# A two-layer recurrent and attention block: the scan's triangle joints cut into pieces of 32 passes between other TensorE products

## The chip, the cores and the metric

The kernel runs on one NeuronCore of a Trainium2 chip. The metric is the device time of one execution, in microseconds (us). Three runs of the kernel before gave 5034.45 to 5045.35 us, median 5039.2 us.

## What is computed

The reference is a block of two layers over 2048 latent rows and 256 context rows of width 1024. Layer 0 is a recurrent mixer (16 heads of 64) that is scanned in both directions; layer 1 is a differential attention over 2304 keys. The change touches only the scan of layer 0, which per head and direction is

```
def step(S, inp):
    r_t, w_t, k_t, v_t, kk_t, a_t = inp
    sa = jnp.einsum("bhvk,bhk->bhv", S, kk_t)
    S = (S * w_t[:, :, None, :]
         - sa[..., None] * (kk_t * a_t)[:, :, None, :]
         + v_t[..., None] * k_t[:, :, None, :])
    return S, jnp.einsum("bhvk,bhk->bhv", S, r_t)
```

## The kernel before, in words

The program runs in phases: projections of layer 0 (`phase1`), the scans (`phase2`), the readout and the projections of layer 1, attention, and the last product. Only `phase2` differs.

`phase2` cuts the 2304 rows into 36 chunks of 64 and treats both directions of a chunk together. Inside a chunk the recurrence is a triangular system of 64 unknowns per head and direction. Its matrix is inverted in blocks: VectorE and GpSimd invert the 32x32 triangles on the diagonal (`invert`, two chunks at a time), four VectorE transposes unpack the result into `Tt` and `Dg` (`unpack`), and two small products of 32x32 blocks join the triangles. The first, `join_rows` (line 743), multiplies the off-diagonal block of `A` with `Tt` for two chunks at once (`w` = 0 and 1). The second, `join` (line 754), multiplies by `U`, which ScalarE has filled with `Dg` times -1 (line 759, four instructions), for one chunk. Each product of `join` or `join_rows` covers 16 heads and two 32x32 blocks; a float32 product is two passes of TensorE, so one joint of one chunk is 64 passes.

The loop variable `m` counts chunks whose scores are made, and `i = m - LEAD` is the chunk whose recurrence runs, five behind. One iteration, a step here, issues for each engine in this written order (`in_order` pins it):

- `chain(i)`, a generator in pieces: products of the state with QR (`xps` and `ops`); KB with RV, then RU with U into `chps` (its negation by ScalarE becomes the new RU, line 820); KB with RU into `xps` (line 825), after which VectorE updates the state `St` (lines 827 and 828); Pb with RU into `ops` (line 833), copied to RV by ScalarE (line 834) and stored. I call them KB·RU and Pb·RU. The first piece, KS with RV, is issued at the end of the step before.
- four groups of score products of chunk `m` (`order[0]` to `order[3]`, line 686, 32 passes each). Two go through `scores_k` (VectorE writes KS), two through `scores_b` (ScalarE copies A, VectorE writes Pb). Every group takes both buffers of the pool `sc` (tiles `scps`).
- eight transposes of BT by TensorE for each direction (`turn_keys`, tiles `chps`), copied to KB by ScalarE.
- the joints. In steps with odd `i` (the variable `even` in the code) it is both `join_rows`, so I call them Tt steps. In steps with even `i` (`odd` in the code) it is `join` of two chunks, one early and one late in the step: U steps. Their tiles are `chps`, in the pool `ch`.

The pools `sc` and `ch` have two buffers each, handed out in turn. SyncE's queue carries the loads of the next chunks and the stores of RV, spread by `pump` over the step. In the last five steps (`more` is false) no scores are left.

Of the kernel before, what the change touches and what calls it, by code (L numbers as in the profile page):

```python
# [11 lines left out]
F32 = mybir.dt.float32  # L12
# [21 lines left out]
def bcast(ap, dim, n):  # L34

    ap = ap.unsqueeze(dim)
    shape = list(ap.shape)
    shape[dim] = n
    return ap.broadcast_to(shape)
# [573 lines left out]
def phase2(k):  # L613
# [9 lines left out]
    with ExitStack() as st:  # L623
# [12 lines left out]
        sc = pool("p2sc", 2, space=PSUM)  # L636
        ch = pool("p2ch", 2, space=PSUM)
# [13 lines left out]
        def pump(n=1):  # L651

            for _ in range(min(n, len(queue))):
                traced = nc.cur_bb.bb.instructions
                queue.pop(0)()
                if i >= 0:
                    at = next(x for x in reversed(traced) if x.engine == mybir.EngineType.Activation)
                    k.tc.add_manual_dep(
                        traced[-1], at.name,
                        mybir.DependencyInfo(mybir.DependencyClass.Sync, mybir.DependencyReason.DATA),  # L660
                        reason="loads spread over the step")
# [76 lines left out]

        parts = ((slice(0, 32), slice(32, 64), slice(32, 64)), (slice(96, 128), slice(64, 96), slice(0, 32)))

        joint = lambda: ch.tile([128, 16, 32], F32, name="chps")

        def join_rows(A, par):

            cs = slice(16 * par, 16 * par + 16)
            ps = joint()
            for h in range(16):
                c = 16 * par + h
                for e, m, uc in parts:
                    nc.tensor.matmul(ps[m, h], A[e, c, uc], Tt[e, c], start=(h == 0), stop=True, skip_group_check=True)  # L750
            for e, m, uc in parts:
                nc.scalar.copy(Tt[m, cs], ps[m])

        def join(par):

            cs = slice(16 * par, 16 * par + 16)
            for g in range(4):
                r = lanes(g)
                nc.scalar.mul(U[r, cs, 32 * (g % 2):32 * (g % 2) + 32], Dg[r, cs], -1.0)
            yield  # L760
            ps = joint()
            for h in range(16):
                c = 16 * par + h
                for e, m, uc in parts:
                    nc.tensor.matmul(ps[e, h], Tt[m, c], U[m, c, uc], start=(h == 0), stop=True, skip_group_check=True)
            for e, m, uc in parts:
                nc.scalar.copy(U[e, cs, uc], ps[e])
            yield
# [9 lines left out]
        def chain(i, QR, KS, Pb, RV, KB):  # L778

            last = i + 1 == NCH  # L780
            par = i % 2
# [33 lines left out]
            for ab in range(2):  # L815
                for p in range(8):
                    for d in range(2):
                        h = 8 * ab + p
# [3 lines left out]
            if not last:  # L822
                for p, ab, h in heads:
                    for d in range(2):
                        add(pS[d][half[ab], p], KB[i, d][half[d], p, ab], RU[half[d], h], False, True)
                for d in range(2):
                    nc.vector.tensor_tensor(St[:, d], pS[d], St[:, d], op=ALU.add)
                    nc.vector.tensor_tensor(St[:, d], St[:, d], bcast(k.dec[:, d, ORDER[d][i]], 2, 64), op=ALU.mult)
            for ab in range(2):
                for p in range(8):  # L830
                    for d in range(2):
                        h = 8 * ab + p
                        add(po[ab][other[d], p], Pb[half[d], h], RU[half[d], h], False, True)
                nc.scalar.copy(RV[:, 8 * ab:8 * ab + 8], po[ab])
            for d in range(2):
                n = ORDER[d][i]
                (nc.sync if i + 2 < NCH else nc.scalar).dma_start(
                    out=S["o"][d, 64 * n:64 * n + 64].rearrange("t (h v) -> t h v", v=64), in_=RV[other[d]])
            yield

        step = lambda g: next(g, None)
        none = iter(())
        mk, mp = causal_masks(k, cx)
        QR, KS, Pb, BK, BT, RV, KB, A = {}, {}, {}, {}, {}, {}, {}, {}
# [27 lines left out]
        inv0, unp, joins, N, chains = none, none, [none, none], {}, {}  # L872

        with in_order(k, mybir.EngineType.PE, mybir.EngineType.DVE, mybir.EngineType.Activation, mybir.EngineType.Pool):
            for m in range(nch + LEAD):
                i, g = m - LEAD, m // 2
                more = m < nch
                par = m % 2

                def turn_keys(d):  # L880
                    if 0 <= i + 1 < nch:
                        KB[i + 1, d] = bt.tile(wide, F32, name=f"KB{d}")
                        turned(d, BT.pop((i + 1, d)), KB[i + 1, d])

                def fill():
                    if not more:
                        step(mods[1])
                    elif i < -1:
                        step(mods[0])
                        step(inv0)  # L890
# [5 lines left out]
                c = chains.pop(i, none)  # L896
# [11 lines left out]
                group = (i + 1) // 2  # L908
                even = i >= -1 and i % 2 == 1 and i + 1 < nch
                odd = i >= 0 and i % 2 == 0  # L910
                if more:
                    KS[m] = kp.tile([128, 16, 2, 64], F32, name="KS")
                    Pb[m] = pp.tile([128, 16, 64], F32, name="Pb")
                    if par == 0:
                        A[g] = ip.tile([128, 32, 64], F32, name="A", bufs=2)
                    args = both(BK, m), both(QR, m)
                    keys = [lambda q=q: scores_k(q, *args, KS[m]) for q in range(2)]
                    rest = [lambda q=q: scores_b(q, *args, A[g], Pb[m], par) for q in range(2)]
                    order = rest + keys if par else keys + rest
                else:  # L920
                    order = [lambda: None] * 4
                if even:
                    unp = unpack(N.pop(group))
                    joins = [join(0), join(1)]
                if odd:
                    step(joins[0])
                order[0]()
                pump(2)
                fill()
                if even:  # L930
                    step(unp)
                step(c)
# [1 line left out]
                order[1]()  # L934
                pump(2)
                fill()
                if more and par == 1:
                    inv = invert(A[g], nc.gpsimd if g else nc.vector)
                    N[g] = step(inv)
                if even:  # L940
                    step(unp)
                step(c)
                pump(2)
                fill()
                if more and par == 1:
                    step(inv)
                if even:
                    for w in range(2):
                        join_rows(A[group], w)
                    A.pop(group)  # L950
                    step(unp)
                if odd:
                    step(joins[1])
                    step(joins[1])
                pump()
                order[2]()
                pump(2)
# [1 line left out]
                    step(unp)  # L959
                if more and par == 1:  # L960
                    step(inv)
                turn_keys(0)
                pump()
                fill()
                order[3]()
# [787 lines left out]
```

## Time and profile before

| | us |
|---|---|
| median of 3 runs | 5039.2 (5034.45 to 5045.35) |
| the profiled execution | 5032.15 |
| its span, first to last instruction | 5030.4 |
| TensorE (PE) busy in the span | 4533.0 (90%) |
| VectorE (DVE) | 3535.2 (70%) |
| ScalarE (ACT) | 2423.8 (48%) |
| GpSimd (POOL) | 1413.0 (28%) |
| mean granted TensorE clock | 0.949 of full |

The scans run from about 1250 us to 2260 us of the span. A granted clock of 1.00 is 2.4 GHz, one of 0.50 is 1.2 GHz. In the waits, "issue" is idle time before an instruction that waited for nothing that the profile shows. Durations of matmuls overlap, so a group of passes is read by its start and its length as a whole.

### The profile page before, as it was taken

The numbers are of one execution on the slowest core, as the hardware profiler recorded it, in microseconds if no ns is written. First come the engines' busy times: TensorE is split into PE (matmuls) and PEld (weight loads), VectorE is DVE, ScalarE is ACT, GpSimd is POOL, SyncE is SP. The second block draws the span as 40 slices with busy tenths as digits, with TensorE's granted clock in tenths as the row PEclk, the third lists the DMA queues.
The fourth block names the chain that finished last, engine by engine and source line by source line (L and its number), as shares of the span: only waits on it lengthen the run. The fifth ranks groups of instructions, "written<-read, shape, count | busy, mean of one in ns | idle before, by whom it ended". The sixth has DMA issues, their size and how long they took to land. (4 is left out here: it accounts for less than half of the span.)

```text
span 5030.4 us, 117428 instructions
## 1 busy us (share of the span) xinstructions
PE 4533.0 (90%) x49938; PEld 4043.9 (80%) x49938; DVE 3535.2 (70%) x5470; ACT 2423.8 (48%) x4098; POOL 1413.0 (28%) x1673
## 2 busy tenths in 40 slices
PE   7999999995777777786879999999999999999999
PEld 5999999992776677665668888878988888898887
DVE  6778777776555555538878448318899899989853
ACT  5555555551444344442342122117777777777730
POOL 1221111111654555423422112022233223323300
PEclk8999999997888988887889999999999999999999
DMA  4565565556455555556653332240111011010042
GB/s 168 161 188 166 171 185 160 167 151 218 137 148 156 148 156 149 157 171 199 204 185 110 106 124 93 92 122 1 28 45 29 17 45 36 27 28 18 10 155 92
DMA packets 642124, 594.30 MB, mean 118 GB/s; under 512 B 30470, under 2 KB 528569, under 8 KB 640577
## 3 DMA queue, kind: packets, MB, share of 16 engines
q1 hardware_dynamic: 639441, 584.16, 38.2%
q8 instruction: 394, 6.46, 0.5%
q10 hardware_dynamic: 2160, 2.62, 0.2%
q14 instruction: 129, 1.06, 0.1%
HBM read 386.91 MB, written 199.77 MB: 117 GB/s over the span
## 5 line engine op out<-in xcount | busy, mean ns | idle before, releaser
L1485 ACT ACTIVATE p<-p,m 128x2304 f32<-128x2304 f32 x256 | 568.8, 2222 | 200.7 <-DVE p L1474 198.6
L1517 PE MATMUL pv<-v,at 128*128 128x128 f32 x4608 | 626.2, 277 | 6.1 <-ACT at L1512 4.3
L1517 PEld LDWEIGHTS pv<-v,at 128*128 128x128 f32 x4608 | 564.3, 192 | 15.8 <-ACT at L1512 12.5
L1471 PE MATMUL sc<-ks,qh 128*128 128x512 f32 (+1 forms) x1280 | 520.2, 406 | 15.2 <-DVE p L1474 15.1
L1472 PE MATMUL sc<-ks,ql 128*128 128x512 f32 (+1 forms) x1280 | 463.7, 371 | 0.3 <-POOL ql L1452 0.3
L363 PE MATMUL mmps<-hH,wH 128*128 128x386 f32 x1632 | 430.8, 344 | 18.5 <-DVE sg L574 12.5
L1512 ACT COPY at<-tps 128x512 f32<-128x512 f32 (+1 forms) x640 | 345.2, 540 | 178.9 <-PE tps L1510 175.1
L1495 DVE SCALAR_TENSOR_TENSOR p<-p,r,p 128x1152 f32<-128x1152 f32 x256 | 427.0, 1668 | 4.5
L363 PE MATMUL mmps<-hL,wH 128*128 128x386 f32 x1632 | 426.5, 341 | 2.1 <-DVE hL L92 2.1
L998 PE MATMUL mmps<-wH,hH 128*128 128x512 f32 x1088 | 424.5, 390 | 3.1 <-ACT hH L91 3.1
L363 PE MATMUL mmps<-hH,wL 128*128 128x386 f32 x1632 | 425.6, 341 | 1.2 <-DVE nm_ss L197 0.8
L998 PE MATMUL mmps<-wL,hH 128*128 128x512 f32 x1088 | 424.2, 390 | 0.0
L998 PE MATMUL mmps<-wH,hL 128*128 128x512 f32 x1088 | 423.7, 390 | 0.0
L1474 DVE TENSOR_SCALAR_CACHE_REDUCE p<-sc,m 128x1280 f32<-128x1280 f32 x256 | 395.5, 1545 | 17.6 <-PE sc L1472 1.5
L1452 POOL TENSOR_TENSOR ql<-qt,qh 128x256 fp32r<-128x256 f32 x128 | 113.5, 886 | 977.8 <-ACT qt L1451 916.5
L1510 PE MATMUL tps<-ident,p 128*128 128x128 f32 x2304 | 361.6, 275 | 10.4 <-ACT qt L1451 5.5
L1474 DVE TENSOR_SCALAR_CACHE_REDUCE p<-sc 128x1024 f32<-128x1024 f32 x256 | 311.5, 1217 | 56.8 <-PE sc L1472 55.6
L710 POOL TENSOR_TENSOR rank<-N 128x130 f32<-128x130 f32 (+14 forms) x442 | 233.4, 528 | 406.7 <-DVE N L711 373.4
L1510 PEld LDWEIGHTS tps<-ident,p 128*128 128x128 f32 x2304 | 273.3, 141 | 61.1 <-ACT at L1512 11.6
L363 PEld LDWEIGHTS mmps<-hH,wH 128*128 128x128 f32 x1632 | 297.7, 191 | 24.4 <-DVE sg L574 16.0
L363 PEld LDWEIGHTS mmps<-hH,wL 128*128 128x128 f32 x1632 | 301.2, 190 | 2.1 <-DVE nm_ss L197 1.2
L363 PEld LDWEIGHTS mmps<-hL,wH 128*128 128x128 f32 x1632 | 300.2, 190 | 3.3 <-DVE hL L92 3.1
(296 smaller groups left out, 10094.9 us busy)
## 6 DMA issues: line engine op xcount, KB each, us to landing
wr<-in_rw_in_dram SPq DMA_DIRECT2D x102, 512.0 KB
s_qr<-QR SPq DMA_DIRECT2D x48, 768.0 KB
QR<-s_qr SPq DMA_DIRECT2D x144, 256.0 KB
BK<-s_bk SPq DMA_DIRECT2D x144, 256.0 KB
BT<-s_bk SPq DMA_DIRECT2D x144, 256.0 KB
s_bk<-BK SPq DMA_DIRECT2D x47, 768.0 KB
wraw<-in_da_in_dram SPq DMA_DIRECT2D x64, 512.0 KB
RV<-s_v SPq DMA_DIRECT2D x72, 256.0 KB
```

Of the source, the lines that this page charges most:

```text
L363: nc.tensor.matmul(a[:, :b1 - b0], wt[:, kt, :], ht[:, kt, b0:b1], start=(kt == 0 and wt is wH and ht is hH), stop=(kt == KT - 1 and last))
L710: eng.tensor_tensor(t, bcast(N[:, m + 1:32, m], 2, m), bcast(N[:, m, 0:m], 1, 31 - m), op=ALU.mult)
L998: k.nc.tensor.matmul(ps, s(kt), m(kt), start=(kt == 0 and s is sH and m is mH), stop=(kt == KT - 1 and last))
L1452: nc.gpsimd.tensor_tensor(ql, qt, qh.bitcast(F32), op=ALU.subtract)
L1471: nc.tensor.matmul(s[:, b0 - g0:b1 - g0], qh[:, cs], ks, start=True, stop=False)
L1472: nc.tensor.matmul(s[:, b0 - g0:b1 - g0], ql[:, cs], ks, start=False, stop=True)
L1474: nc.vector.tensor_scalar(tiles[n][c][:, g0:g1], s[:, :g1 - g0], -1.0, m, op0=ALU.mult, op1=ALU.min, accum_out=least)
L1485: nc.scalar.activation(P, P, AF.Exp, bias=m, scale=-1.0, accum_out=z)
L1495: nc.vector.scalar_tensor_tensor(P0[:, b0:b1], P1[:, b0:b1], r, P0[:, b0:b1], op0=ALU.mult, op1=ALU.add)
L1510: nc.tensor.transpose(ps[:, c - b0:c - b0 + 128], P0[:, c:c + 128], k.ident)
L1512: (eng.copy if eng is nc.scalar else eng.tensor_copy)(at[b][:, :b1 - b0], ps[:, :b1 - b0])
L1517: nc.tensor.matmul(acc, at[b][:, c - b0:c - b0 + 128], H.v[:, c // 128], start=(c == 0), stop=(c == T - 128))
```

## The change

`join_rows` and `join` become generators that stop after 8 of 16 heads, so each joint is two pieces of 32 passes. The pieces go between other products of the step. The tiles of three of the four joints move from the pool `ch` to `sc`. `chain` gets two more stops, before Pb·RU and between its two halves. In a U step the four instructions that negate `Dg` for the second chunk are issued right behind `order[1]`, ahead of the two RV copies. `turn_keys(0)` moves ahead of the last piece, and so ahead of `order[2]` and `order[3]`.

```diff
-        joint = lambda: ch.tile([128, 16, 32], F32, name="chps")
+        joint = lambda keys: (sc if keys else ch).tile([128, 16, 32], F32, name="scps" if keys else "chps")
 
         def join_rows(A, par):
 
             cs = slice(16 * par, 16 * par + 16)
-            ps = joint()
+            ps = joint(more)
             for h in range(16):
                 c = 16 * par + h
                 for e, m, uc in parts:
                     nc.tensor.matmul(ps[m, h], A[e, c, uc], Tt[e, c], start=(h == 0), stop=True, skip_group_check=True)
+                if h == 7:
+                    yield
             for e, m, uc in parts:
                 nc.scalar.copy(Tt[m, cs], ps[m])
+            yield
...
-            ps = joint()
+            ps = joint(more and par == 1)
             for h in range(16):
                 c = 16 * par + h
                 for e, m, uc in parts:
                     nc.tensor.matmul(ps[e, h], Tt[m, c], U[m, c, uc], start=(h == 0), stop=True, skip_group_check=True)
+                if h == 7:
+                    yield
...
+            yield
             for ab in range(2):
                 for p in range(8):
                     for d in range(2):
                         h = 8 * ab + p
                         add(po[ab][other[d], p], Pb[half[d], h], RU[half[d], h], False, True)
                 nc.scalar.copy(RV[:, 8 * ab:8 * ab + 8], po[ab])
+                if ab == 0:
+                    yield
...
+                rows = [none, none]
                 if even:
                     unp = unpack(N.pop(group))
                     joins = [join(0), join(1)]
+                    rows = [join_rows(A[group], w) for w in range(2)]
                 if odd:
                     step(joins[0])
                 order[0]()
                 pump(2)
                 fill()
+                if odd:
+                    step(joins[0])
                 if even:
                     step(unp)
                 step(c)
...
                 order[1]()
                 pump(2)
                 fill()
+                if odd:
+                    step(joins[1])
...
                 step(c)
                 pump(2)
+                step(rows[0])
+                step(c)
+                step(rows[0])
+                if odd:
+                    step(joins[1])
+                step(c)
+                step(rows[1])
                 fill()
                 if more and par == 1:
                     step(inv)
+                last = rows[1], joins[1] if odd else none
+                if not more:
+                    for w in last:
+                        step(w)
+                turn_keys(0)
+                for w in last:
+                    step(w)
+                A.pop(group if even else None, None)
                 if even:
-                    for w in range(2):
-                        join_rows(A[group], w)
-                    A.pop(group)
                     step(unp)
-                if odd:
-                    step(joins[1])
-                    step(joins[1])
                 pump()
                 order[2]()
...
-                turn_keys(0)
                 pump()
                 fill()
                 order[3]()
```

What moves is shown at three places, each as the built programs have it. A row of TensorE counts products; a float32 product is two passes, a transpose (`ident`) one.

TensorE in a Tt step, from the end of KB·RU (`xps<-RU,KB`) to the first KS products of the next chunk. Before:

```order
L782 MATMUL xps<-RU,KB_24280 64x64
L782 MATMUL ops_24213<-RU,Pb 64x64 x16
L782 MATMUL ops_24214<-RU,Pb 64x64 x16
L750 MATMUL chps<-Tt,A 32x32 x64
L686 MATMUL scps<-QR,BK 64x128 x16
L775 MATMUL chps<-ident,BT 128x128 x8
L686 MATMUL scps<-QR,BK 64x128 x16
```

And with the change:

```order
L787 MATMUL xps<-RU,KB_25350 64x64
L750 MATMUL scps<-Tt,A 32x32 x16
L787 MATMUL ops_25283<-RU,Pb 64x64 x16
L750 MATMUL scps<-Tt,A 32x32 x16
L787 MATMUL ops_25284<-RU,Pb 64x64 x16
L750 MATMUL scps<-Tt,A 32x32 x16
L780 MATMUL chps<-ident,BT 128x128 x8
L750 MATMUL scps<-Tt,A 32x32 x16
L686 MATMUL scps<-QR,BK 64x128 x32
```

The first piece of the joint now stands ahead of Pb·RU, and the two last score groups stand side by side, with the joint's own `scps` tiles right before them.

TensorE in a U step, the same stretch, with the change (before, the order was KB·RU, both `ops` groups, `chps<-U,Tt` x32, a score group, the eight transposes, a score group):

```order
L787 MATMUL xps<-RU,KB_24862 64x64
L787 MATMUL ops_24795<-RU,Pb 64x64 x16
L768 MATMUL scps<-U,Tt 32x32 x16
L787 MATMUL ops_24796<-RU,Pb 64x64 x16
L780 MATMUL chps<-ident,BT 128x128 x8
L768 MATMUL scps<-U,Tt 32x32 x16
L686 MATMUL scps<-QR,BK 64x128 x32
```

Here one joint takes one `scps` buffer, and the score group behind it takes both.

ScalarE in a U step, from the negation of RU to the KB copies. Before:

```order
L820 ACTIVATE RU<-chps 128x512 x2
L698 COPY A<-scps 128x256 x2
L834 COPY RV<-ops_21585 128x512
L834 COPY RV<-ops_21586 128x512
L759 ACTIVATE U<-Dg 32x16x32 x4
L767 COPY U<-chps 32x16x32 x2
L776 COPY KB_22036<-chps 128x512 x2
```

And with the change:

```order
L825 ACTIVATE RU<-chps 128x512 x2
L698 COPY A<-scps 128x256 x2
L762 ACTIVATE U<-Dg 32x16x32 x4
L840 COPY RV<-ops_21585 128x512
L840 COPY RV<-ops_21586 128x512
L781 COPY KB_21994<-chps 128x512 x2
L772 COPY U<-scps 32x16x32 x2
```

The four negations stand ahead of the RV copies, and the first two KB copies ahead of the U copies. On SyncE's queue one load of QR per step passes ahead of the two stores of RV; VectorE's and GpSimd's order is unchanged.

## Rows read from the trace of the kernel before

**Rows 1.** Waits of TensorE, 1256 to 2256 us: us in total, times, longest.

```profile
PE xps L782 <- issue: 52.3, 48, 2.7
...
PE chps L765 <- ACT U L759: 41.9, 36, 2.2
...
PE chps L750 <- DVE Tt L732: 4.9, 6, 3.1
```

**Rows 2.** Windows: stretch, length, busy us (instructions) of PE, PEld, DVE, ACT, POOL; clock.

```profile
1256.00:2256.00 1000.00, 778.60 (x27466) 697.41 (x27466) 530.69 (x691) 418.43 (x776) 497.02 (x908) 0.88 0.52 151
...
2020.50:2027.30 6.80, 6.22 (x108) 5.28 (x112) 3.35 (x4) 2.99 (x6) 0.00 (x0) 0.50 0.70 191
2027.40:2051.20 23.80, 17.71 (x777) 16.44 (x769) 18.56 (x24) 6.96 (x13) 14.54 (x24) 1.00 0.54 158
```

**Rows 3.** Timeline of TensorE, one U step: start, length, instructions, [idle before].

```profile
2015.98 0.58 PE L782 MATMUL xps<-RU,KB 64*64 64x64 f32 x24 [1.01 <-issue]
2016.39 2.03 PE L782 MATMUL ops<-RU,Pb 64*64 64x64 f32 x64
2020.41 0.26 PE L765 MATMUL chps<-U,Tt 32*32 32x32 f32 x2 [1.99 <-ACT U L759]
...
2023.26 1.98 PE L686 MATMUL scps<-QR,BK 64*64 64x128 f32 x32
...
2027.07 1.20 PE L686 MATMUL scps<-QR,BK 64*64 64x128 f32 x32
...
2030.07 1.09 PE L775 MATMUL chps<-ident,BT 128*128 128x128 f32 x8
```

**Rows 4.** Timeline of ScalarE in the same stretch.

```profile
2014.31 0.65 ACT L698 COPY A<-scps 128x256 f32<-128x256 f32 x2 [0.19 <-PE scps L686]
...
2019.09 2.57 ACT L759 ACTIVATE U<-Dg 32x512 f32<-32x512 f32 x4
2023.37 1.16 ACT L767 COPY U<-chps 32x512 f32<-32x512 f32 x2 [1.71 <-PE chps L765]
2026.32 0.58 ACT L776 COPY KB<-chps 128x512 f32<-128x512 f32 x1 [1.79 <-PE chps L775]
```

**Rows 5.** Timeline of VectorE, the Tt step that follows.

```profile
2041.75 1.29 DVE L693 TENSOR_TENSOR KS<-scps,causalK 128x512 f32<-128x512 f32 x2 [2.32 <-PE scps L686]
2043.05 1.94 DVE L732 STREAM_TRANSPOSE Tt<-N 32x1024 f32<-32x1024 f32 x1
...
2051.84 0.76 DVE L699 TENSOR_TENSOR Pb<-scps,causalP 128x256 f32<-128x256 f32 x2 [1.44 <-ACT A L698]
```

**Rows 6.** Timeline of TensorE, the same Tt step.

```profile
2041.48 1.18 PE L782 MATMUL xps<-RU,KB 64*64 64x64 f32 x62
...
2044.20 1.50 PE L782 MATMUL ops<-RU,Pb 64*64 64x64 f32 x44 [0.91 <-issue]
2045.63 1.51 PE L750 MATMUL chps<-Tt,A 32*32 32x32 f32 x83
2049.32 0.89 PE L750 MATMUL chps<-Tt,A 32*32 32x32 f32 x45 [2.18 <-issue]
2050.13 1.10 PE L686 MATMUL scps<-QR,BK 64*64 64x128 f32 x32
2051.17 1.96 PE L775 MATMUL chps<-ident,BT 128*128 128x128 f32 x8
2053.05 1.85 PE L686 MATMUL scps<-QR,BK 64*64 64x128 f32 x32
```

**Rows 7.** Timeline of TensorE: one idle stretch among wide products.

```profile
1311.42 1.09 PE L782 MATMUL ops<-RU,Pb 64*64 64x64 f32 x30 [2.07 <-issue]
```

**Rows 8.** Timeline of TensorE: one idle stretch inside a joint.

```profile
1370.88 1.41 PE L750 MATMUL chps<-Tt,A 32*32 32x32 f32 x71 [1.26 <-issue]
```

**Rows 9.** Windows around the two idle stretches, columns as in Rows 2.

```profile
1307.20:1313.90 6.70, 4.63 (x227) 4.42 (x220) 6.36 (x7) 1.38 (x3) 5.95 (x10) 1.00 0.62 158
...
1372.00:1375.30 3.30, 3.30 (x50) 2.90 (x44) 2.69 (x4) 2.20 (x6) 2.99 (x5) 0.50 0.78 225
```

## The prediction

> **What bounds the kernel now.** I read the windows first, because the change touches only the scans. From 1256 to 2256 us TensorE is busy for 778.60 of 1000 us, far ahead of the others (VectorE 530.69), at a mean granted clock of 0.88 [rows 2]. As the clock has two levels, 1.00 and 0.50, it ran at the low one for about 240 of these 1000 us. So the scans are a sequence on TensorE, stretched by idle time and by a low clock, and the reader should look for these two.
>
> The waits come next. Idle time that nothing in the profile explains ("issue") leads, 52.3 us ahead of `xps` alone; the joint in the U steps waits 41.9 us for the negation of `Dg` on ScalarE, which is 2.3 us in each of 18 steps; the Tt joint waits for VectorE's last transpose only 4.9 us in all [rows 1].
>
> Then the timeline of one pair of steps. In the U step KB·RU ends at 2016.56 us, Pb·RU at 2018.42, and the joint cannot start until 2020.41, since the negations start only at 2019.09, behind the RV copies [rows 3, 4]. From 2020.5 to 2027.3 the clock is 0.50: a score group takes 1.98 us against 1.10 at 1.00 [rows 2, 3, 6]. The last score group ends at 2028.27, 11.7 us after KB·RU. In the Tt step KB·RU ends at 2042.66 and the last score group at 2054.90, 12.2 us later, with 0.91 and 2.18 us of issue idle inside and the low clock again for transposes and scores (1.96 and 1.85 us, against 1.09 and 1.10 at full clock) [rows 3, 6]. Between the two idle moments lie 44 + 83 = 127 passes [rows 6]: this idle time looks like the supply of the next instructions, and a wait elsewhere can hide it.
>
> **The change, U step** (16 with scores). The negations follow the A copies, so they start at 2014.96; three of four, which the joint needs, are done 1.9 us later, at 2016.9, half a microsecond before the first half of Pb·RU (2.03 / 2 = 1.0 us) would end [rows 3, 4]. Without the 1.01 us of idle ahead of KB·RU it would be a wait of 0.5. I take 0.2 between 0 and 0.5, and the old 2.3 us wait is gone.
>
> What is late next is the score group. It takes both `scps` buffers, one of which the joint has just filled, and now nothing stands between them: its second product waits for the two U copies (1.16 us), which may stand behind a KB copy (0.58) [rows 4]. I take 1.4 between 1.16 and 1.75, the low end being likelier because the KB copy mostly ends with the last piece. The last score group then follows the one before it without the eight transposes that used to separate them, so VectorE's two KS products (1.29 us [rows 5]) are no longer hidden: 1.35, between 0.7 and 2.
>
> With the whole stretch at full clock it is 1.0 + 0.2 + 0.58 (32 passes, from 83 in 1.51 [rows 6]) + 1.0 + 1.09 + 0.58 + 1.4 + 1.10 + 1.35 + 1.10 = 9.4 us, against 11.7 that held low clock: 2.3 saved. The early joint is split too; its U copies now queue behind two A copies (0.65 + 1.16 us [rows 4]), and RU·U waits for them after 1.0 us of KB·RV. I charge 0.3 between 0 and 0.8. Net, before any clock charge: -2.0.
>
> **The Tt step** (15 in the steady state). The first piece stands right behind KB·RU, but needs VectorE's transpose, done at 2044.99, because that stands behind two KS products that wait for the score group [rows 5]. KB·RU ends at 2042.66, so TensorE stands still for 2.3 us, and Pb·RU, which used to cover this, is queued behind the wait. Then 0.58 + 1.0 + 0.58 + 1.0 + 0.58 + 1.09 + 0.58 = 5.4. The score group waits for the two last Tt copies: 1.16 us, with an RV and two KB copies ahead of them on ScalarE, 1.4 between 1.16 and 2.3. 1.10 for the scores; then A copies (0.65) and Pb (0.76), no longer covered by transposes, 1.25 between 0.7 and 1.4 [rows 4, 5]; 1.10. Sum 12.6. The 3.1 us of issue idle is mostly hidden by these waits; I leave 0.4, between 0 and 2.2. So 13.0 at full clock against 12.2 that held low clock: +0.75, before any clock charge.
>
> **The clock.** Each microsecond at 0.50 costs 0.45 us where TensorE is dense (1.98 for 1.10, 1.96 for 1.09 [rows 3, 6]), about half of that over the KS products, whose issue idle it hides, and nothing over a wait. Two places show what comes before a fall. An idle stretch of 2.07 us among wide products left the clock at 1.00 through 1313.9; one of 1.26 us inside a joint of 32x32 blocks was followed by 0.50 [rows 7 to 9]. So the narrow joints count little, and spreading them helps, but the new idle stretches (2.3, 1.4 and 1.25 in a Tt step) hurt. I expect 2 us at low clock in the stretch of a U step, 1.5 of it over the last scores and KS (0.35), and 4 us in that of a Tt step, 1.3 on the dense pieces (0.6), 1.1 at half price (0.25), the rest on waits. The charges are chosen; the rivals take them at zero and in full.
> The Trainium skill, TensorE: Matmul & The Clock Gate, section "Why this matters for your kernels", puts a fall down to idle gaps between bursts of matmuls. By that rule alone the shape of the joints would not matter; the rows 7 to 9 above disagree, since the longer gap left the clock up. By it the U step would lose its falls and every Tt step would keep one at its 2.3 us wait, and the sum would be +2 us instead of -4.
>
> **The rest.** The two U steps without scores lose their wait of about 2 us each: -4. The first Tt step gains the two waits at the scores: +2.5. On SyncE's queue one QR load passes the two stores of RV; I price it at nothing, since in these rows TensorE waits for copies, transposes and issue, not for loads [rows 1, 3, 6], and a load is used a step later; if that cover were gone, the score groups would wait for it. VectorE's order stays.
>
> **Sum.** 16 x (-2.0 + 0.35) = -26.4; 15 x (0.75 + 0.85) = +24; -4 + 2.5. Total -4 us. The profiled execution took 5032.15 us, 1.75 more than its span and 7 less than the median of the runs shown, so 5028 there is 5035 for a median. A measurement of this kernel can tell about 0.2%, 10 us, from no change: my forecast is **no measurable change**, own range 5017 to 5053.
>
> **Rivals.**
> - The clock holds. The pieces keep it at 1.00 through the whole stretch. For it: wide products stand between all pieces. Against: three idle stretches per step. Without clock charges: 16 x -2.0 + 15 x 0.75 - 1.5 = -22, with the waits at their low ends -37: 5013, down to 4998. Faster.
> - The Tt step's wait decides. The piece behind KB·RU waits 2.3 us for VectorE, the clock falls there, and Pb·RU, the pieces and the transposes run at 0.50. For it: VectorE's chain is fixed by the score group, not by TensorE's order [rows 5]. Tt charge 1.9 instead of 0.85, U charge 1.4: 16 x -0.6 + 15 x 2.65 - 1.5 = +29: 5068. It decides from a Tt charge of about 1.5 per step on, if the U step keeps only half of its gain. Slower.
> - Idle gaps alone govern the clock (a mechanism without regard to the width of products): U steps -2.0, Tt steps 0.75 + 1.6 (3.5 us of dense pieces at 0.50). 16 x -2.0 + 15 x 2.35 - 1.5 = +2: 5041. The page named above would have it so; rows 7 to 9 speak against it.
> - The change does not do what it says: the pieces meet supply idle of the same length wherever they stand, since 127 passes come between two such moments anyhow, and the gain and the loss both vanish: 5039.
>
> **Chances.** Forecast 0.36 (of which faster 0.10, same 0.18, slower 0.08); clock holds 0.28 (faster 0.26, same 0.02); Tt wait decides 0.22 (slower 0.20, same 0.02); idle alone 0.08 (same 0.05, slower 0.02, faster 0.01); no effect 0.06 (same 0.03, faster 0.02, slower 0.01). Together faster 0.39, same 0.30, slower 0.31. The range reaches from the low end of the first rival to just past the second: 4998 to 5070.
>
> **What would show it.** In the new profile: no wait of the U joint over 0.7 us; a wait of about 2.3 us of the Tt joint for VectorE in nearly every Tt step, some 34 us in all; waits of the scores for Tt and U copies and for KS and Pb, each about 1.3 us and together some 80 us; less issue idle; and a mean clock in the scans above 0.88, about 0.92. If the clock is over 0.96, the first rival holds; if it stays near 0.88, the second. The forecast is wrong if the waits of the scores are missing, or if the Tt joint's wait is under 1 us.

## The result and the profile after

The changed kernel takes 5101.51 us (median of 4 runs, 5092.93 to 5103.55) beside 5042.27 us of the kernel before on the same chip (4 runs, 5034.45 to 5048.05): a ratio of 1.0115, 95% interval 1.0096 to 1.0135. It is slower by about 59 us, and outside the range that was forecast. The profiled execution took 5103.55 us, with a span of 5101.8.

Line numbers move by a few: the U joint is L768 now (L765 before), the chain's products L787 (L782), the transposes of KB L780 (L775), the copies of Tt and U L754 and L772. The Tt joint (L750), the scores (L686), KS (L693), Pb (L699) and the transpose into Tt (L732) keep theirs.

The loss lies in the 31 steps that have scores. The windows run from the first copy to `seen` (one per step) to the 32nd. Columns: stretch, length, busy us (instructions) of PE, PEld, DVE, ACT and POOL, then the granted clock, DMA share, GB/s. First the kernel before:

```profile
1268.20:2146.20 878.00, 677.51 (x24305) 620.89 (x24305) 492.74 (x646) 366.05 (x684) 456.68 (x837) 0.88 0.53 151
```

The same 31 steps of the changed kernel:

```profile
1277.90:2214.70 936.80, 752.47 (x24305) 676.57 (x24306) 492.08 (x646) 364.75 (x682) 453.73 (x831) 0.83 0.48 142
```

936.8 - 878.0 = 58.8 us, as much as the medians differ by. (The spans of these two profiled executions differ by 71.4 us; 9.7 of it lie ahead of the first of these steps and 2.9 behind the last.) The same 24305 passes kept TensorE busy for 75 us more, while VectorE's and ScalarE's work did not change. The clock fell from 0.88 to 0.83: the time at the low level (0.50) went from 204.8 to 317.7 us, by the clock records of the two traces. TensorE's idle time fell, from 200.1 to 183.4 us (the sum of the rows of the wait view). So over these steps the change lost nothing by standing still; it lost by running at the low clock: half of the 112.9 us that were added there, 56.5 us, would account for it.

The waits of TensorE in the changed kernel over these steps (engine, tile, line, what it waited for: us in total, times, longest):

```profile
PE xps L787 <- issue: 27.8, 33, 1.5
PE ops L787 <- issue: 25.8, 20, 3.1
PE scps L750 <- DVE Tt L732: 24.2, 15, 2.2
...
PE scps L686 <- DVE Pb L699: 13.9, 15, 0.9
PE scps L686 <- DVE KS L693: 13.0, 19, 0.8
PE scps L686 <- ACT U L772: 12.8, 15, 0.9
PE scps L686 <- ACT Tt L754: 11.1, 15, 0.9
...
PE scps L768 <- ACT U L762: 4.0, 9, 1.6
```

[rows 1] covers more than these steps. In the same 31 steps the kernel before has:

```profile
PE xps L782 <- issue: 49.8, 45, 2.7
...
PE chps L765 <- ACT U L759: 37.8, 32, 2.0
...
PE chps L750 <- DVE Tt L732: 1.8, 5, 0.5
```

So these are the waits that the prediction listed. The U joint's 37.8 us for ScalarE is 4.0. The Tt joint's 1.8 us for VectorE is 24.2, in every Tt step. The scores wait in four places, 50.8 us together. Issue idle ahead of `xps` is down from 49.8 to 27.8 us.

One Tt step of the changed kernel on TensorE (start, length, instructions, [idle before]), beside [rows 6]:

```profile
2045.39 0.80 PE L787 MATMUL xps<-RU,KB 64*64 64x64 f32 x37 [0.62 <-issue]
2046.12 0.24 PE L750 MATMUL scps<-Tt,A 32*32 32x32 f32 x2
2047.66 0.69 PE L750 MATMUL scps<-Tt,A 32*32 32x32 f32 x30 [1.29 <-DVE Tt L732]
2048.27 1.15 PE L787 MATMUL ops<-RU,Pb 64*64 64x64 f32 x32
2049.35 0.78 PE L750 MATMUL scps<-Tt,A 32*32 32x32 f32 x27
2050.78 0.32 PE L750 MATMUL scps<-Tt,A 32*32 32x32 f32 x5 [0.65 <-issue]
2051.03 1.97 PE L787 MATMUL ops<-RU,Pb 64*64 64x64 f32 x32
2052.93 1.06 PE L750 MATMUL scps<-Tt,A 32*32 32x32 f32 x32
2053.92 1.97 PE L780 MATMUL chps<-ident,BT 128*128 128x128 f32 x8
2055.82 1.06 PE L750 MATMUL scps<-Tt,A 32*32 32x32 f32 x32
...
2058.15 1.98 PE L686 MATMUL scps<-QR,BK 64*64 64x128 f32 x30 [0.65 <-ACT Tt L754]
2061.05 2.10 PE L686 MATMUL scps<-QR,BK 64*64 64x128 f32 x29 [0.92 <-DVE Pb L699]
...
2062.93 0.43 PE L686 MATMUL scps<-QR,BK 64*64 64x128 f32 x3
```

And its clock, by windows with the columns from above:

```profile
2046.20:2049.60 3.40, 2.10 (x79) 1.88 (x81) 3.33 (x4) 0.13 (x1) 3.01 (x6) 1.00 0.93 228
2049.60:2066.70 17.10, 14.88 (x325) 13.14 (x318) 6.99 (x8) 8.34 (x16) 15.20 (x25) 0.50 0.47 142
```

The wait of 1.29 us stands two passes into the first piece. Two microseconds after it the clock falls, and it stays low for 17 us: most of the second piece, the second half of Pb·RU, the other two pieces, the transposes (1.97 us where full clock gives 1.09), both score groups and KS·RV of the next step. KB·RU ends at 2046.2 and the last score group at 2063.4, 17.2 us later with 13.7 of them at the low clock, against 12.2 us in [rows 6]. The mean over the 15 Tt steps, between the same two ends, is 16.5 us with 11.4 of them at the low clock, against 12.3 and 5.2 before. For the 16 U steps it is 12.5 with 4.5, against 11.9 and 5.6, and 1.9 us of low clock more in the KS·RV behind, which was always at full clock.

### The profile page after: what moved, and what is told of

The parts are those of the page before. It is cut to its first block, busy times and chain, and to the rows that moved or that the text cites. A ratio compares the mean times of both kernels' runs of the same rounds, so it can differ in the third digit from the quotient of the medians.

```text
span 5101.8 us, 117333 instructions
## 1 busy us (share of the span) xinstructions
PE 4613.3 (90%) x49938; PEld 4103.9 (80%) x49938; DVE 3538.4 (69%) x5470; ACT 2427.6 (48%) x4098; POOL 1413.7 (28%) x1673
## 5 line engine op out<-in xcount | busy, mean ns | idle before, releaser
L1496 DVE TENSOR_SCALAR_CACHE_REDUCE p<-sc,m 128x1280 f32<-128x1280 f32 x256 | 395.6, 1545 | 17.2 <-PE sc L1494 1.3
L686 PE MATMUL scps<-QR,BK 64*64 64x128 f32 x4608 | 253.2, 333 | 99.0 <-DVE Pb L699 21.6
L686 PEld LDWEIGHTS scps<-QR,BK 64*64 64x64 f32 x4608 | 188.7, 166 | 152.1 <-issue 44.2
## 6 DMA issues: line engine op xcount, KB each, us to landing
QR<-s_qr SPq DMA_DIRECT2D x144, 256.0 KB
BK<-s_bk SPq DMA_DIRECT2D x144, 256.0 KB
BT<-s_bk SPq DMA_DIRECT2D x144, 256.0 KB
RV<-s_v SPq DMA_DIRECT2D x72, 256.0 KB
```

The source lines that it names most:

```text
L686: nc.tensor.matmul(f2(out[ab][(other if key else half)[d], j]), BK[d][rows, p, 1 - d if key else d], f2(QR[d][rows, p]), start=(j == 0), s ...
L1496: nc.vector.tensor_scalar(tiles[n][c][:, g0:g1], s[:, :g1 - g0], -1.0, m, op0=ALU.mult, op1=ALU.min, accum_out=least)
```

## The experiments

My theory after the result: the first piece's wait for VectorE, and the scores' waits for their buffers, draw out the low clock of the Tt steps; the pieces themselves do no harm. The rivals: the pieces as such lower the clock; or the waits simply cost their length. All ratios are to the kernel before on the same chip.

**Signs alone.** The kernel before, with only the negations moved.

```diff
                 order[1]()
                 pump(2)
                 fill()
+                if odd:
+                    step(joins[1])
...
                 if odd:
                     step(joins[1])
-                    step(joins[1])
```

> The kernel before with one edit: the four negations of the second joint of U are issued behind KB·RU, ahead of the RV copies; all joints stay undivided, where they were and in their old buffers. If the U joint's wait for ScalarE, 2.3 us in each of 18 U steps, was really paid, it goes (under 0.3 us each) and the time falls by 16 to 18 times 1.6 to 2.3 us, to 5000 to 5015 us. If the supply of instructions takes the place of the wait (one stop every 127 passes or so, which the wait hid), the issue idle in the U steps grows by as much as the wait falls and the time stays within 10 us of the kernel before, 5033 to 5052.

Measured: 5020.76 us, ratio 0.9975 [0.9964, 0.9986], 13 us faster: between the two theories. Its waits in the 31 steps:

```profile
PE scps L686 <- issue: 32.9, 24, 2.5
PE chps L765 <- issue: 25.5, 15, 3.0
```

The wait for ScalarE (37.8 us before) is gone from the list. But issue idle ahead of the same joint is now 25.5 us (11.9 before, in the same steps) and ahead of the scores 32.9 (19.3). All idle together is 192.5 us against 200.1. So four fifths of the wait came back as supply, as the rival said. What was gained is clock: 47.8 us less at the low level (table below), 5.6 to 2.7 us in a U stretch.

**U steps alone.** The changed kernel, with the Tt joint as before.

```diff
-            ps = joint(more)
+            ps = joint(False)
...
-                if h == 7:
-                    yield
...
-                    rows = [join_rows(A[group], w) for w in range(2)]
...
+                if even:
+                    for w in range(2):
+                        join_rows(A[group], w)
```

(and `turn_keys(0)` back behind `order[2]` in Tt steps.)

> The changed kernel with its U steps as they are, and the joint of Tt as in the kernel before: undivided, behind Pb·RU, in its old buffer. If the loss sits in the Tt steps (the wait of the first piece for VectorE, and the low clock behind it), the Tt stretch is back at 12.3 us and the time is 5040 to 5056 us, that of the kernel before or up to 14 us above it. If the pieces as such lower the clock, in U steps as much as in Tt steps, about half of the loss of 59 us stays: 5066 to 5078.

Measured: 5031.6 us, 0.9987 [0.9978, 0.9996]. Slightly faster than before, and faster than both theories gave, so U steps alone make no loss. The Tt stretch is back at 12.4 us. By whole steps the U step is 28.9 us here against 28.5 before, and the Tt step, with its work as before, 27.1 against 28.2: time moves between neighbouring steps, so the length of one kind of step does not show by itself what an edit in it cost.

**Tt steps alone.** The reverse: `join` undivided in `chps` and in its old places, `join_rows` as in the change.

> The changed kernel with its Tt steps as they are, and the joints of U as in the kernel before: undivided, with the negations behind the RV copies, in their old buffer. If the loss sits in the Tt steps, it is nearly whole: 5080 to 5100 us, with about 11 us at the low clock in each Tt stretch of 16.5 us. If both kinds of step share it, 5066 to 5078.

Measured: 5091.38 us, 1.0112 [1.0095, 1.0129], the whole loss, with 11.0 us of low clock in a Tt stretch of 16.7. What remained was to say which part of the Tt step.

**Early transpose.** The changed kernel, with VectorE's second transpose into Tt ahead of the KS products.

```diff
+                if even:
+                    step(unp)
                 order[1]()
...
-                if even:
-                    step(unp)
                 step(c)
```

> The changed kernel with one edit: VectorE's second transpose into Tt, for which the first piece of the Tt joint waits 1.0 to 2.2 us behind KB·RU, is issued ahead of the KS products instead of behind them, into a gap of VectorE. If that wait is what lowers the clock of the Tt steps, the wait falls under 0.3 us, the low clock in a Tt stretch from 11.4 to about 6 us, the stretch from 16.5 to about 13.5 us, and the time to 5045 to 5065. If the pieces and the waits of the scores for their buffers keep the clock low by themselves, the wait goes and the clock does not come back: 5085 to 5105.

Measured: 5079.86 us, 1.0077 [1.0064, 1.009]. The wait is gone (no row of L750 for L732 is left), the low clock in a Tt stretch is 5.1 us and the stretch 14.3 us. The clock came back as the wait theory said, but the time only by (1.0115 - 1.0077) x 5040 = 19 us, a third of the loss, and between my two theories (5045 to 5065, 5085 to 5105). Still there were the waits of the scores:

```profile
PE scps L686 <- DVE Pb L699: 13.9, 15, 0.9
PE scps L686 <- DVE KS L693: 13.2, 20, 0.8
PE scps L686 <- ACT U L772: 12.8, 15, 0.9
PE scps L686 <- ACT Tt L754: 12.2, 15, 0.9
```

**The wait alone.** The kernel before, with the undivided Tt joint moved up.

```diff
                 step(c)
                 pump(2)
+                if even:
+                    for w in range(2):
+                        join_rows(A[group], w)
+                    A.pop(group)
+                step(c)
                 fill()
```

(with a `yield` in `chain` ahead of Pb·RU, and the old call removed.)

> The kernel before with the undivided joint of Tt moved up behind KB·RU, ahead of Pb·RU, in its old buffer; no piece, no other edit. The wait for VectorE's transpose stands alone here. If it lowers the clock for longer than the joint's own narrow products did (the low clock then starts about 3 us behind KB·RU instead of 5), the Tt stretch grows from 12.3 us to between 13.5 and 15 us and the time to 5055 to 5080 us. If the wait only takes the place of the 2.3 us of issue idle, and the clock falls once per step in either order, 5028 to 5048.

Measured: 5047.14 us, 1.0017 [1.0005, 1.0029]: about 9 us slower, at the upper end of what the rival gave. Its wait for VectorE is larger than in the change (29.3 us in 15 steps), yet without pieces behind it and without waits at the scores it costs little. The low clock in a Tt stretch is 6.1 us.

**The buffers alone.** The kernel before, with the late joints in `scps`.

```diff
-        joint = lambda: ch.tile([128, 16, 32], F32, name="chps")
+        joint = lambda keys: (sc if keys else ch).tile([128, 16, 32], F32, name="scps" if keys else "chps")
```

(with `joint(more)` and `joint(more and par == 1)` at the two calls, as in the change.)

> The kernel before with the late joints in the buffers of the scores (scps instead of chps), undivided and in their old place, as the changed kernel has it; the transposes of KB stay between the two score groups. If the waits of the first score group for the copies out of the joint (0.7 to 0.9 us each in the changed kernel) are paid in full, each of 31 steps loses about 0.8 us: 5055 to 5070. If they take the place of issue idle, 5030 to 5050.

Measured: 5058.33 us, 1.0042 [1.0027, 1.0057]: 21 us slower, as the first theory had it. Two rows are new, apart from single waits:

```profile
PE scps L686 <- ACT U L767: 11.9, 16, 0.9
...
PE scps L686 <- ACT Tt L752: 10.2, 17, 0.9
```

The sum of all idle time did not change (199.7 us against 200.1), so these waits too stand where issue idle stood. The low clock grew by 51 us.

**Pieces in the old buffers.** The early transpose kept; all joints in `chps`, the transposes of KB between the score groups.

```diff
-        joint = lambda keys: (sc if keys else ch).tile([128, 16, 32], F32, name="scps" if keys else "chps")
+        joint = lambda keys: ch.tile([128, 16, 32], F32, name="chps")
...
                 last = rows[1], joins[1] if odd else none
-                if not more:
-                    for w in last:
-                        step(w)
-                turn_keys(0)
                 for w in last:
                     step(w)
...
                 order[2]()
...
+                turn_keys(0)
```

> The changed kernel with the early transpose of the run before (no wait of the first Tt piece), and with the joints back in their old buffers and the transposes of KB back between the two score groups (no waits of the scores for joints, KS or Pb). Only the pieces are left, and the early signs. If the two kinds of wait made the whole loss, the time is that of the kernel with the signs alone, 5010 to 5032. If pieces among the products lower the clock by themselves, it is 5045 to 5070.

Measured: 5013.41 us, 0.9948 [0.9932, 0.9964]: 26 us faster than before and 84 faster than the change, with every piece in place. Without the new waits the pieces do no harm that can be told from the signs alone (0.9975), which are part of this kernel. Its 31 steps:

```profile
1265.40:2126.20 860.80, 683.69 (x24305) 620.09 (x24305) 493.49 (x647) 365.37 (x684) 458.86 (x840) 0.90 0.53 154
```

**Undivided U joints with Tt pieces.** The same, with `join` undivided behind Pb·RU as in the run with the signs alone.

> The kernel with the signs alone (undivided joints of U), and the Tt joint in pieces around the halves of Pb·RU with the early transpose, all in the old buffers. If pieces without waits spread the narrow products and raise the clock of the Tt steps, the low clock in a Tt stretch falls under 4 us from 5.4 and the time to 4995 to 5012; if pieces do nothing by themselves, it is that of the signs alone, 5015 to 5028; if they lower the clock, above 5035.

Measured: 5015.06 us, 0.9953 [0.9939, 0.9968]. The forecast of the pieces that do nothing by themselves holds by its number, which is level with the run before it. Against the signs alone it is 11 us less, but its 31 steps are no shorter (858.3 us against 855.3) and the Tt stretch is 12.5 us against 12.4; whether Tt pieces bring anything stays open.

**Back to the change, one edit at a time.** Two runs put one part each back into the run with pieces in the old buffers: the first only the line of `joint` (late joints in `scps`), the second only the place of the transposes, ahead of both score groups:

```diff
+                turn_keys(0)
                 A.pop(group if even else None, None)
...
-                turn_keys(0)
```

> The run with pieces in their old buffers, and one edit: the late joints go to the buffers of the scores. The transposes of KB stay between the two score groups. That kernel lies 65 us under the one with both the buffers and the transposes moved. If the buffers make most of it, because the first score group waits for the copies of the joint right behind it, 5055 to 5075; if they cost what they cost alone in the kernel before (21 us there), 5028 to 5044, and the move of the transposes makes the rest.

Measured: 5041.22 us, 1.0007 [0.9997, 1.0018]: level with the kernel before. The buffers cost (1.0007 - 0.9948) x 5037 = 30 us here, not most of the 65; by its number the second theory holds.

> The run with pieces in their old buffers, and one edit: the transposes of KB go ahead of both score groups, so that these follow each other. (They need the buffers of the joints, so they wait for the joints' copies, which the changed kernel avoids.) If two score groups in a row, the second waiting for VectorE's KS products or Pb, make the 40 us and more that the buffers alone don't explain, 5045 to 5070; if the cover of the transposes is worth nothing because issue idle stands there anyway, 5008 to 5025.

Measured: 5064.34 us, 1.0052 [1.0037, 1.0066], 52 us above its base. The rows that came:

```profile
PE scps L686 <- DVE KS L693: 14.2, 25, 0.8
PE scps L686 <- DVE Pb L699: 14.0, 15, 0.9
PE chps L780 <- ACT U L772: 7.3, 16, 0.7
PE chps L780 <- ACT Tt L754: 5.1, 14, 0.7
```

The first two are the uncovered waits of the second score group. The other two are of this kernel's own making (transposes behind joints in the same buffers), so 52 us is an upper bound for the move. In the change's buffers the move costs what lies between 1.0077 and 1.0007, 35 us. Not all of this is clock. TensorE's idle time in the 31 steps grows with the move, from 176.2 to 195.3 us here and from 170.0 to 182.0 us in the change's buffers, so a part of these waits was paid by standing still.

**The late transpose.** The same base, with VectorE's transpose back behind KS.

> The run with pieces in their old buffers, and one edit: VectorE's second transpose into Tt back behind the KS products, where the changed kernel has it, so that the first piece waits 1 to 2 us behind KB·RU. If the wait costs by itself what it cost in the changed kernel (16 to 22 us), 5028 to 5037; if it costs much there only because waits of the scores follow it within the same low clock, it costs what it cost alone in the kernel before (8 us) or less, 5010 to 5024.

Measured: 5028.91 us, 0.9982 [0.9973, 0.9991]: 17 us above its base, the first theory. By the times the wait costs about as much here as in the change (19 us), more than the 9 us it cost ahead of an undivided joint. The low clock in a Tt stretch rises from 5.3 to 7.3 us. With the waits at the scores behind it the same edit took it from 5.1 to 11.4 us (early transpose and the change). So in the profiles the wait draws out the low clock far more where the waits at the scores follow, which is the second theory; that the times show no such difference (17 and 19 us, known to some 9 and 12 us) stays unexplained.

**The wait filled.** The changed kernel, with ten transposes of the identity where it stood idle. They are overwritten by the joint, so the result is the same.

```diff
             ps = joint(more)
+            if more and par == 0:
+                wide = ps.rearrange("p (a b) c -> p a (b c)", a=4)
+                for j in range(10):
+                    nc.tensor.transpose(wide[:, j % 4], ident, ident)
```

> The changed kernel with ten wide transposes of the identity, whose results are overwritten, issued behind KB·RU ahead of the first piece of the Tt joint, in its buffer: 1.4 us of useless products at full clock in the place of the wait for VectorE, which stays as the piece's condition. The computation is as in the changed kernel. If it is the idle time in that place that brings the clock down, the low clock in a Tt stretch falls from 11.4 to 6 to 8 us and the time lies 10 to 25 us under that of the changed kernel, about that of the run with the early transpose: 5070 to 5086. If the clock falls because of the narrow pieces that follow, whatever stands ahead of them, the low clock stays at 10 us or more and the time at 5088 to 5105, or above that by what the transposes exceed the wait.

Measured: 5053.81 us, 1.0033 [1.0016, 1.0049]: (1.0115 - 1.0033) x 5040 = 41 us faster than the change, by adding work, and more than I had expected. Its eight runs spread more than those of the others (5044.27 to 5082.93), and the profiled one is the slowest of them. Even there the low clock in a Tt stretch is 5.9 us on average instead of 11.4. The wait was not filled in every step; this much of it is left:

```profile
PE scps L754 <- DVE Tt L732: 10.2, 12, 1.0
```

Three of the 15 Tt stretches have no low clock at all; in the change none is without. This is one of the three, and it had no wait left:

```profile
1669.98 1.31 PE L750 MATMUL scps<-ident 128*128 128x128 f32 x10
1671.22 0.94 PE L754 MATMUL scps<-Tt,A 32*32 32x32 f32 x32
1672.09 1.15 PE L791 MATMUL ops<-RU,Pb 64*64 64x64 f32 x32
...
1679.06 1.10 PE L686 MATMUL scps<-QR,BK 64*64 64x128 f32 x30 [0.92 <-ACT Tt L758]
1681.08 1.32 PE L686 MATMUL scps<-QR,BK 64*64 64x128 f32 x29 [0.92 <-DVE Pb L699]
```

Its window:

```profile
1670.00:1682.50 12.50, 10.29 (x290) 8.78 (x291) 8.27 (x9) 5.20 (x10) 11.17 (x18) 1.00 0.72 183
```

The same pieces and the same two waits at the scores as in the step shown of the changed kernel, but no idle time behind KB·RU: the clock stays at 1.00 and the stretch takes 12.5 us instead of 17.2. The mean of the 15 stretches is 15.5 against 16.5. Step by step the rest of the wait does not decide: the other two stretches at full clock had 0.8 and 0.9 us of it left, and two with 0.2 and 0.4 us left were at the low clock for 12 and 13 us. Nor is it shown that filling the gap is all that the transposes do. The run with the early transpose has no such wait either (issue idle of 11.6 us stands ahead of its Tt pieces, 8.3 here), and its ratio, 1.0077, is 22 us above this one. What ten dense products do for the clock beyond filling a gap was not separated; they were not tried together with the early transpose.

All kernels side by side. Lengths are of the 31 steps; idle is TensorE's; low is the time at the low clock, which is also 2 x (1 - clock) x length of the window, apart from rounding.

| kernel | ratio to before | 31 steps, us | idle, us | low, us |
|---|---|---|---|---|
| before | 1 | 878.0 | 200.1 | 204.8 |
| the change | 1.0115 | 936.8 | 183.4 | 317.7 |
| signs alone | 0.9975 | 855.3 | 192.5 | 157.0 |
| U steps alone | 0.9987 | 869.2 | 174.3 | 194.6 |
| Tt steps alone | 1.0112 | 923.6 | 197.8 | 297.0 |
| early transpose | 1.0077 | 904.6 | 182.0 | 235.5 |
| wait alone | 1.0017 | 887.1 | 204.2 | 221.9 |
| buffers alone | 1.0042 | 902.1 | 199.7 | 256.0 |
| pieces, old buffers | 0.9948 | 860.8 | 176.2 | 167.3 |
| and U undivided | 0.9953 | 858.3 | 190.9 | 153.6 |
| pieces, score buffers | 1.0007 | 876.5 | 170.0 | 208.2 |
| pieces, keys moved | 1.0052 | 906.4 | 195.3 | 218.5 |
| pieces, late transpose | 0.9982 | 867.1 | 170.2 | 187.7 |
| wait filled | 1.0033 | 912.8 | 177.2 | 211.8 |

The length less half of the low time is 772 to 782 us in eleven of the 14 kernels: there the clock is nearly the whole difference. It is 787 us with the early transpose and 797 with the keys moved, where waits were also paid as time, and 807 with the wait filled, which holds 20 us of added transposes.

## Why the prediction was wrong

**The failed step is the clock charge**, in both kinds of step: "2 us at low clock in the stretch of a U step" (0.35) "and 4 us in that of a Tt step" (0.85). That is 16 x 2 + 15 x 4 = 92 us in the 31 stretches. They hold 16 x 4.5 + 15 x 11.4 = 243, against 16 x 5.6 + 15 x 5.2 = 168 before, and the low clock runs on behind them. So it grew where the sum had it shrink. By whole steps, the Tt step is 31.2 us against 28.2, +3.1 where +0.75 + 0.85 = +1.6 stood: 23 us of the miss over 15 steps. The U step is 29.25 us against 28.5, +0.75 where -1.65 stood: 38 us over 16 steps. 15 x 3.1 + 16 x 0.75 = 58.5, the loss. Since time moves between neighbouring steps, the two runs with one kind of step alone are the better account: U steps alone came to -6.5 us where the sum had -26.4 - 4 = -30.4, Tt steps alone to +56 where it had 24 + 2.5 = +26.5. Each kind of step makes about half of the miss.

**A second term of the U step failed with it.** The -2.0 us counted the removed wait as time won. In the run with the signs alone four fifths of that wait came back as issue idle, and the 13 us that it won were won by the clock.

**The sum at full clock** was about right for a Tt stretch. It gave 13.0 us; the three of the last experiment that held 1.00 took 12.5, 12.7 and 13.5, with 1.3 us of added transposes in the place of the wait. For a U stretch it gave 9.4, and the three that held 1.00 in that run took 10.0, 10.0 and 11.0, about 1 us more. So I had the stalls nearly right, and took too little for what they do to the clock.

**The waits** came where they were forecast, with smaller sizes: 24.2 us for VectorE's transpose (34 forecast), 50.8 us at the scores (80; they are 72 if each is counted from the start of the product before it). The U joint's wait was to stay under 0.7 us; eight of nine did, and one took 1.6. Issue idle fell, as forecast. TensorE waits for no load in these steps, so pricing the moved load at nothing held. The mean clock, forecast at 0.92, is 0.83; by the test that I set ("near 0.88, the second") it speaks for the second rival, and more.

**The second rival** ("the Tt step's wait decides") had the mechanism for one part of three. The chain of single edits from the pieces in the old buffers to the change gives the prices: 30 us for the late joints in the scores' buffers (0.9948 to 1.0007), 35 for the transposes moved ahead of the scores (to 1.0077), 19 for the wait of the first piece (to 1.0115). The start of the chain, signs and pieces, is worth -26. -26 + 30 + 35 + 19 = 58. The 31 steps of the single profiles give 16, 28, 32 and -17 for the same edits. Both ways the waits at the scores weigh more, together, than the one that the rival named; which of the three is the largest stays open. The rival's price, 5068, was too low as well.

**"The clock holds"** failed on the clock: no kernel here held it. Without the new waits the pieces leave the mean clock of the 31 steps at 0.90, above the 0.88 before, but the signs alone give 0.91. The rival's 5013 and 4998 are also 4 us too low, since its -22 and -37 were counted from the forecast's 5035 and not from 5039, from which the other rivals are counted.

**"The change does not do what it says"** was right on idle time: in all 14 kernels TensorE's idle time in the 31 steps lies between 170 and 204 us, whichever wait was removed or added. A removed wait comes back for the most part as issue idle, and an added one mostly hides it. The traces also bear out the supply that the prediction suspected behind its 127 passes: in the kernel before, in the change and with the signs alone, the stops of over 0.6 us that count as issue (109, 78 and 126 of them) lie 127 or 128 passes apart, or a few times that, without exception.

**Idle gaps and the rule.** I had set the Trainium skill, TensorE: Matmul & The Clock Gate, section "Why this matters for your kernels", against [rows 7 to 9] and held that the narrow joints bring the clock down more than a gap does. By that rule a fall follows idle gaps between bursts. The section speaks of longer gaps than those in the timelines shown here, so neither those rows nor these runs test the rule itself, and the +2 us of my sum are not the section's. The early transpose and the filled wait go its way: same narrow pieces, the wait for VectorE gone or smaller, 5.1 and 5.9 us low instead of 11.4. But the amount of idle time does not order the kernels in the table (the change has less than the kernel before), and the wait alone, ahead of an undivided joint, cost about 9 us. What the runs show is that a gap right ahead of the cut joints, with gaps close behind them, prolongs the low clock on average; how the chip weighs gaps, narrow products and dense ones was not separated further.

## What to carry to other kernels

Where TensorE's instruction supply or its clock sets the pace, price a moved wait by what it does to the granted clock of the stretch behind it, and not by its length alone: sum the idle time over all steps first, and if it stays the same, look at the clock. Cut narrow products into pieces only if no piece gets a new dependence or another product's buffer; here the pieces with the early transpose and in their old buffers take 0.9948 of the time before (0.9975 of it without any pieces, by the signs alone), and the same pieces with the waits 1.0115. Keep work that covers a buffer's hand-over (the transposes between the two score groups) where it is.

## What the runs showed that I had not expected

- Ten useless transposes in each of 16 steps, 1.3 us each time, made the changed kernel 41 us faster; the clock stayed up in part of the steps.
- A low clock can run on through more than half of a step: 17.1 us at 0.50 in the step shown, while TensorE was busy for 14.9 of them.
- Moving a product's destination to another pool of the same size cost 21 us without moving a single instruction of TensorE, and without more idle time: 51 us more at the low clock.
- The first score product starts 1156.3 to 1171.4 us after the start of the span in the 14 profiles, and no edit touches what runs before it. A difference of 15 us between two single profiles says nothing by itself, so the 31 steps were compared, and the ratios. The 31 steps of one profile are a single execution too, and in the chain of edits above they differ from the ratios by 7 to 14 us.
